# A hybrid encoder trunk on one core: unit order at the end of gate/up, a root by ScalarE, and earlier spawns

## The chip, the cores and the metric

One Trainium2 chip, one core of it. The metric is the device time of one execution in microseconds; it is taken as the median over several runs. A profile is one more execution, recorded instruction by instruction.

## The reference

One layer over 2048 tokens of width 1024, in float32. The kernel has to compute:

```python
h = rmsnorm(r, norm1_g)
proj = h @ w_in                        # q, k, v, z, beta, alpha, lx, lg
dn_out  = gated delta rule, both directions, 4 heads of 128, normed, times silu(z)
lru_out = rmsnorm(gelu(lg) * (rglru forward + rglru backward))     # 512 wide
r = r + concat([dn_out, lru_out]) @ w_out
h2 = rmsnorm(r, norm2_g)
gate = dwconv(h2 @ ffn_wg, ffn_conv_w) + ffn_conv_b                # 3 taps along the tokens, 2816 wide
r = r + (gelu(gate) * (h2 @ ffn_wu)) @ ffn_wd
pg = sigmoid(rmsnorm(r, ple_norm_g) @ ple_wg + ple_bg)
r = r + pg * (p @ ple_wp)              # p: 2048 x 256
out = rmsnorm(r, final_g)
```

## The kernel before

**A planner writes the order.** The program is a set of generators ("tasks") that a small list scheduler, `Sched`, runs while the program is built. A task yields `st(...)` with the cost that its next instruction is expected to have on an engine, `W(name)` to wait for an event that another task fires, or `M(sizes)` to wait for memory. `Sched` always takes the task whose next step could start first (plus 20 ns for each step of its priority; a lower number goes first) and issues its instructions. Each engine then executes its instructions in exactly that order. SP issues all DMAs, in order too, so a DMA that has to wait holds those issued behind it. Costs and events change only the order; on the chip, semaphores follow the data.

**Memory** is one arena of 207 KB a partition. A request is refused while there is no free block of its size, or while a task of lower priority number is waiting for memory.

**Precision.** A float32 operand is split into an f16 high and low part: ScalarE writes the high one, VectorE the low one (`split`, lines 1677 and 1679 without a scale, 1681 and 1683 with one). A product is three f16 matmuls. The large products save one in eight by a seven-product scheme: four blocks give seven operands (`operands`; three are blocks as they are, four are sums that POOL forms at line 1706), and `product` runs seven products a unit, 12 matmuls each for gate/up, 30 for down (line 1727). PSUM has banks of 128x512; each product's bank is evicted by ScalarE (line 1944) or VectorE (line 1949) for gate/up, by VectorE (line 2203) for down.

**The stages that the change touches.**

- *The output projection*, in two halves: `out_dn` over the delta rule's heads, then `out_lru` over the recurrence's 512 columns, 16 token tiles each in the order `TILES` (7, 8, 6, 9, ... 0, 15), 24 matmuls a tile (`mm`, line 456). `out_lru` has a `fetcher` that reads the rows of `catl` from DRAM with a transposing DMA (line 1622) into nine buffers. The products are added to the residual `r` by `out_add` (line 1584). The weights of each half are prepared by `out_weights` (`wprep`: loads at line 552, squares at 573 or 576, splits at 602 and 606).
- *The passage to gate/up.* `norm_pairs` takes the token tiles in eight pairs: squares by ScalarE (line 1786), the reciprocal root by `rsqrt` on VectorE alone (lines 373 to 393: an integer guess and three corrections), the scaling into `hb` (line 1794), then seven operands. Pairs 0 to 3 reach their transposed form by DMA (line 1822), pairs 4 to 7 by TensorE (`turned`, line 639) and a ScalarE copy (line 1811). `pair_weights` prepares the weights of the 22 gate/up tiles, gate (even n) and up (odd n) in turn; from n = 1 on it waits for the event `last pair`.
- *Gate/up.* `ffn` runs 44 units (n, u): weight tile pair n, half u of the tokens. `units` overlaps two units in the order 1, (3, 7 of the one before), 2, 5, (4 of the one before), 6. When both halves of gate tile pair j are there, `gate_tile` does the convolution (lines 1994, 1996, 1998) and the gelu (line 2002); `mult` multiplies by up on POOL (line 2012); `act_post` scales and splits the result and stores it to `actd` (line 2047). Three blocks of 8 KB (`blk`) hold gate and up in turn; `room` waits until the one to be written is free.
- *The seam.* At `pdone 20` (the end of unit 20, 1) four tasks start: `p_weights` prepares the 256x1024 weights of `p @ ple_wp`, and three `down_weights` tasks load `w_d` (line 2168) into one raw block of 8 KB each, take seven 2 KB pieces and split into them, one of eleven row blocks after the other. Behind gate/up `p_products` computes `p @ ple_wp` (32 groups of six matmuls; evictions at lines 2418 and 2421, stores to `ppd` at 2424), and then `down_first` runs down's first unit block by block (line 2301, 210 matmuls; `actd` loads at 2276), with 24 matmuls for the eleventh block at its end. `down_unit`'s `load` takes the 16 KB of a ring for the residual's rows when `p_products` ends.

ScalarE's functions come from tables; changing between sets shows as ACT_TABLE_LOAD rows.

Of the kernel before, what the change touches and what calls it, by code (L numbers as in the profile page):

```python
# [16 lines left out]
S = SEQ = 2048  # L17
# [284 lines left out]
def W(*name):  # L302
    return ("w", name)


def M(*sizes, high=False):
    return ("m", sizes, high)
# [48 lines left out]
class Kern:  # L356
# [11 lines left out]
    def rsqrt(self, ss, n, mul, add, outscale, y, tmp):  # L368

        nc = self.nc  # L370
        v, t = tmp[:, 0:n], tmp[:, n : 2 * n]
        yield st(dve=75 + n)
        nc.vector.tensor_scalar(v, ss, mul, add, op0=ALU.mult, op1=ALU.add)
        yield st(dve=75 + n)
        nc.vector.tensor_single_scalar(t.bitcast(I32), v.bitcast(I32), 1, op=ALU.logical_shift_right)
        yield st(dve=75 + n)
        nc.vector.tensor_scalar(y.bitcast(I32), t.bitcast(I32), -1, 0x5F3759DF, op0=ALU.mult, op1=ALU.add)

        yield st(dve=75 + n)
        nc.vector.tensor_tensor(t, y, y, op=ALU.mult)  # L380
        yield st(dve=135 + n)
        nc.vector.scalar_tensor_tensor(t, t, -0.5, v, op0=ALU.mult, op1=ALU.mult)
        yield st(dve=135 + n)
        nc.vector.scalar_tensor_tensor(y, t, 1.5, y, op0=ALU.add, op1=ALU.mult)
        yield st(dve=75 + n)
        nc.vector.tensor_tensor(t, y, y, op=ALU.mult)
        yield st(dve=75 + n)
        nc.vector.tensor_tensor(t, t, v, op=ALU.mult)
        yield st(dve=210 + 2 * n)
        nc.vector.scalar_tensor_tensor(v, t, -10.0 / 3, t, op0=ALU.add, op1=ALU.mult)  # L390
        nc.vector.tensor_scalar(y, y, 0.375 * outscale, None, op0=ALU.mult)
        yield st(dve=135 + n)
        nc.vector.scalar_tensor_tensor(y, v, 5.0, y, op0=ALU.add, op1=ALU.mult)

    def pow2_scale(self, ss, n, target, s, inv, tmp):

# [1196 lines left out]
    def out_weights(self, i):  # L1593
# [13 lines left out]
            nc.vector.tensor_scalar(w.inv, w.inv, 2.0 ** -11, None, op0=ALU.mult)  # L1607
        S.fire("wo%d" % i)

    def out_lru(self):  # L1610

        nc, S = self.nc, self.S
        n = 9
        tiles = yield M(*[2 * KB] * n)

        def fetcher():
            for j, t in enumerate(TILES):
                yield W("catl", t)
                if j >= n:
                    yield W("cat used", j - n)  # L1620
                yield ahead(1400)
                nc.sync.dma_start_transpose(tiles[j % n].f16(8, 128), self.catl[t * 128 : t * 128 + 128, :])
                S.fire("cat", j)

        S.spawn(fetcher(), PR["cat"])
        yield W("wo1")
        w = self.w["wo1"]
        for j, t in enumerate(TILES):
            yield W("cat", j)
            v = tiles[j % n].f16(8, 128)  # L1630
            yield W("r", t // 4)
            for m in range(2):
                cs = slice(m * 512, m * 512 + 512)
                pairs = [(v[:, o + k], a[:, k, cs]) for o, a in ((0, w.hi), (4, w.hi), (0, w.lo)) for k in range(4)]
                b = yield from self.mm(pairs)
                S.spawn(self.out_add(t, m, b, w.inv, "r"), 3)
            S.fire("cat used", j)
            if j + n >= 16:
                tiles[j % n].free()
        for x in self.hlo[1]:  # L1640
            x.free()
# [112 lines left out]
    def norm_pairs(self):  # L1754
# [21 lines left out]
        def begin(i):  # L1776
            ts = TILES[2 * i : 2 * i + 2]
            for t in ts:
                for m in range(2):
                    yield W("r", t, m)  # L1780
            smb = self.A.alloc(64)
            sm = smb.f32(16)
            ss, y, tmp = sm[:, 0:2], sm[:, 4:6], sm[:, 8:12]
            for k, t in enumerate(ts):
                yield st(act=c_act(D))
                nc.scalar.activation(self.junk.b16(D), self.rt(t), AF.Square, accum_out=ss[:, k : k + 1])
            yield from self.rsqrt(ss, 2, 1.0 / D, EPS, HS, y, tmp)
            (hb,) = yield M(8 * KB)
            if i == 7:
                S.fire("last pair")  # L1790
            hv = hb.f32(2, D)
            for k, t in enumerate(ts):
                yield st(dve=c_stt(D))
                nc.vector.scalar_tensor_tensor(hv[:, k], self.rt(t), y[:, k : k + 1], g, op0=ALU.mult, op1=ALU.mult)  # L1794
            smb.free()
            for t in ts:
                yield ahead(1456)
                nc.sync.dma_start(self.rd[:, t * D : t * D + D], self.rt(t))
                self.A.release(self.r[t // 4].off + t % 4 * 4 * KB, 4 * KB)
            u, o = i // 4, min(ts) % 4 * 128  # L1800
            if i % 4 == 0:
                self.hU[u] = yield M(*[8 * KB] * 7)
                S.fire("hT", u)
            yield W("hT", u)
            v = [hv[:, k, z * 512 : z * 512 + 512] for z in range(2) for k in range(2)]
            if i >= 4:
                for x in v:
                    b = yield st(pe=4 * 160, bank=1, lag=H2L)
                    P = self.turned(x, b)
                    yield st(act=c_act(512))  # L1810
                    nc.scalar.activation(x, P, AF.Copy)
                    S.release(b)

            def put(n, x):
                if i >= 4:
                    to = self.hU[u][n].f16(8, 512)[:, :, o : o + 128]
                    yield from self.split(x.rearrange("p (a n) -> p a n", n=128), to[:, 0:4], to[:, 4:8], 512)
                    return
                j, buf = yield from ring.take()
                yield from self.split(x, buf.f16(512), buf.f16(512, at=KB), 512)  # L1820
                yield st(dma=1400)
                nc.sync.dma_start_transpose(self.hU[u][n].f16(8, 512)[:, :, o : o + 128], buf.f16(1024))
                ring.done(j)

            yield from self.operands(("h2", i), RIGHT, v, 512, put)
            yield W(("h2", i), "ops")
            hb.free()
            left[0] -= 1
            if left[0] == 4:
                S.fire("h2", 0)  # L1830
            if not left[0]:
                S.fire("h2", 1)
                for x in sb + [gb]:
                    x.free()
# [66 lines left out]
    def gu_unit(self, n, u):  # L1901
# [22 lines left out]
        def room(i):  # L1924

            if x:
                k = self.rot(j)[0 if u else 2]
                if u:
                    yield W("conv", j, 0)
                else:  # L1930
                    yield W("mul", j - 1, 1) if j else W("blk")
# [131 lines left out]
    def ffn(self):  # L2063
# [15 lines left out]
        def clear():  # L2079
            for u in range(2):  # L2080
                yield W("mul", 10, u)
            for b in self.blk:
                b.free()
            yield W("act", 10)
            for b in self.ab + self.aring.bufs:
# [16 lines left out]

            return f

        todo = [(n, u) for n in range(22) for u in range(2)]
        yield from self.units([begin(n, u) for n, u in todo])
        S.fire("gu end")

# [49 lines left out]
    def down_weights(self, par):  # L2158


        nc, S = self.nc, self.S
        yield W("pdone", 20)
        (raw,) = yield M(8 * KB)
        js = RAWS[par]
        for j in js:
# [2 lines left out]
            nc.sync.dma_start(v, self.io["w_d"][256 * j : 256 * j + 256, :].rearrange("(i p) n -> p i n", p=128))  # L2168
            yield W("wd scale", 8 if j == 10 else 0)
            w = self.wd[j] = yield M(*[2 * KB] * (4 if j == 10 else 7))  # L2170
            blocks = [v[:, i, z * 512 : z * 512 + 512] for i in range(2) for z in range(2)]
            put = lambda n, x, w=w, j=j: self.split(x, w[n].f16(512), w[n].f16(512, at=KB), 512, self.asc[:, j : j + 1])
            if j == 10:
# [8 lines left out]
    def down_unit(self, i):  # L2182
# [6 lines left out]
        def load():  # L2189
            if i == 0:  # L2190
                yield W("pp end")
                self.rring = Ring(S, "r pairs", (yield M(8 * KB, 8 * KB)))
            U.n, U.r = yield from self.rring.take()
            for k, t in enumerate((i, 15 - i)):
# [192 lines left out]

    def p_weights(self):
        nc, io, S = self.nc, self.io, self.S
        yield W("pdone", 20)  # L2390
        hp = yield M(4 * KB, 4 * KB, 4 * KB, high=True)
        sg = hp.pop()
        yield from self.wprep("wp", io["ple_wp"].rearrange("(k p) n -> p k n", p=128), 2, D, None, (hp, [sg]), pieces=2)
        sg.free()
        self.wpb = hp
        yield W("phl")
        yield st(dve=80)
# [156 lines left out]
    def main(self):  # L2554
# [61 lines left out]
        S.spawn(self.p_pairs(), 9)  # L2616

        parts = (self.out_dn, self.out_lru)
        yield from parts[PARTS[0]]()

        def norms():
# [4 lines left out]
            self.mix.free()  # L2626

        S.spawn(norms(), 3)
        S.spawn(self.norm_pairs(), PR["norm"])
        S.spawn(self.pair_weights(), PR["pw"])  # L2630
        yield from parts[PARTS[1]]()
        S.spawn(self.row_squares(), 0)
        self.fsb = A.alloc(128)
# [12 lines left out]
    def go(self):  # L2646
        A, c, io = self.A, self.c, self.io
        S = self.S = Sched(A, range(2, 8))
        self.w, self.wd, self.xc, self.gl, self.zb, self.dp, self.hd, self.acc, self.act = {}, {}, {}, {}, {}, {}, {}, {}, {}
        self.rn, self.hlo, self.pw = {}, {}, {}  # L2650
        self.r, self.hU = [None] * 4, [None] * 2
        self.xT = [A.alloc(16 * KB) for _ in range(4)]
        self.junk = A.alloc(2 * KB, high=True)
# [135 lines left out]
```

## Time and profile before

| | us |
|---|---|
| median of three runs | 2758.08 (2755.16 to 2760.72) |
| the profiled execution | 2759.3 |
| its span, first to last instruction | 2757.4 |
| TensorE busy | 2561.9 (93%) |
| VectorE busy | 1867.5 (68%) |
| ScalarE busy | 1479.5 (54%) |
| GpSimd busy | 825.2 (30%) |
| granted TensorE clock, mean | 0.975 |

PE is TensorE's matmuls and PEld its weight loads, DVE is VectorE, ACT is ScalarE, POOL is GpSimd, SP is SyncE. A row of a stage gives, for each engine, busy time and the number of instructions in brackets. A row of waits gives the engine and line that waited, what released it, the sum in us, how often and the longest. A row of a group gives line, engine, operation, shapes and count, then busy time and mean ns of one, then the engine's idle time before them and what ended it. A row of the timeline gives start, duration, engine, line, and the idle time before in brackets. Busy times of small VectorE rows overlap: one is recorded until its result is written.

### The profile page before, as it was taken

Reading aid. Unit: us, or ns where it says so; the run is one execution under the profiler, and the core shown is the slowest. Engines: PE = TensorE matmul, PEld = TensorE weight load, DVE = VectorE, ACT = ScalarE, POOL = GpSimd, SP = SyncE. Lnnn points to the kernel's source line nnn. Section 1 sums busy time; section 2 is a strip of 40 time slices with the busy share of each in tenths; the row PEclk is TensorE's granted clock in tenths of the full one; section 3 lists DMA queues with packets and bytes.
Section 4 is the critical chain, followed back from the end, with each engine's and each line's share of the span. In section 5 each row is a group of like instructions: output and inputs, shape, how many; then the busy total and the mean of one; then the engine's idle time right before and its main releaser. Section 6 shows DMA issues by size and latency. Waiting matters only on the chain.

```text
span 2757.4 us, 40429 instructions
## 1 busy us (share of the span) xinstructions
PE 2561.9 (93%) x14072; PEld 1311.3 (48%) x14072; DVE 1867.5 (68%) x3902; ACT 1479.5 (54%) x3110; POOL 825.2 (30%) x618
## 2 busy tenths in 40 slices
PE   7998898898989998896999999999996799999998
PEld 4554454456656665443444444444442344444443
DVE  8668977976785667598667777778759832222458
ACT  6676677574747765245666666666646500101323
POOL 1133534736141000034345544444446400000000
PEclk9999999999999999998999999999999999999999
DMA  5332152366544468672223233333225844447973
GB/s 194 73 103 62 54 150 69 93 183 189 151 142 139 132 208 277 157 204 79 77 85 107 89 107 105 106 105 106 92 86 180 255 164 150 166 160 232 271 187 141
DMA packets 433595, 388.20 MB, mean 141 GB/s; under 512 B 158704, under 2 KB 362480, under 8 KB 433392
## 3 DMA queue, kind: packets, MB, share of 16 engines
q1 hardware_dynamic: 433392, 385.62, 46.8%
q8 instruction: 111, 1.82, 0.3%
q14 instruction: 92, 0.75, 0.1%
HBM read 230.34 MB, written 128.97 MB: 130 GB/s over the span
## 4 chain that ended last, share of the span: by engine, by line
PE 53%; DVE 6%; DMA 1%; ACT 1%; issue 1%; POOL 0%; SPq 0%; DVEq 0%; ACTq 0%
PE P L1727 40%; PE P L456 12%; DVE arena L1683 2%; DVE arena L1679 1%; PE P L2301 1%; DVE arena L1794 1%; DVE arena L1584 0%; DMA ppd<-arena 0%; DMA arena<-in_w_d_dram 0%; DMA arena<-catl 0%; DMA arena<-actd 0%; ACT arena L1681 0%; POOL arena L1706 0%; PE P L1452 0%; DVE arena L2418 0%
## 5 line engine op out<-in xcount | busy, mean ns | idle before, releaser
L1727 PE MATMUL P<-arena 128*128 128x512 f16 x5166 | 1127.2, 380 | 15.7 <-ACT arena L1944 9.8
L456 PE MATMUL P<-arena 128*128 128x512 f16 x4224 | 983.6, 384 | 32.2 <-ACT arena L2421 10.1
L1727 PEld LDWEIGHTS <-arena 128*128 128x128 f16 x5166 | 507.1, 98 | 624.1 <-issue 25.6
L456 PEld LDWEIGHTS <-arena 128*128 128x128 f16 x4224 | 413.6, 99 | 487.3 <-issue 47.0
L1683 DVE SCALAR_TENSOR_TENSOR arena<-arena 128x512 f16<-128x512 f32 (+2 forms) x408 | 449.5, 1133 | 118.6 <-ACT arena L1681 118.3
L1706 POOL TENSOR_TENSOR arena<-arena 128x512 f32<-128x512 f32 (+1 forms) x200 | 352.5, 1776 | 507.6 <-DVE arena L1683 358.4
L1681 ACT ACTIVATE arena<-arena 128x512 f16<-128x512 f32 (+2 forms) x408 | 283.0, 723 | 294.7 <-POOL arena L1706 139.8
L2203 DVE SCALAR_TENSOR_TENSOR arena<-P,arena 128x512 f32<-128x512 f32 x95 | 70.1, 750 | 225.9 <-PE P L1727 190.2
L2012 POOL TENSOR_TENSOR arena<-arena 128x512 f32<-128x512 f32 x88 | 136.3, 1569 | 241.2 <-ACT arena L2002 175.6
L2254 ACT ACTIVATE arena<-arena 128x1024 bf16<-128x1024 f32 x16 | 16.9, 1057 | 246.8 <-DVE arena L2203 237.8
L1944 ACT ACTIVATE arena<-P 128x512 f32<-128x512 f32 x176 | 102.5, 587 | 80.7 <-PE P L1727 76.1
L738 DVE SCALAR_TENSOR_TENSOR arena<-P,arena 128x511 f32<-128x511 f32 (+1 forms) x192 | 140.7, 743 | 1.9
L1261 POOL TENSOR_TENSOR arena<-arena 128x512 f32<-128x512 f32 x64 | 118.4, 1865 | 58.8 <-DVE arena L1211 46.8
L1949 DVE TENSOR_TENSOR arena<-P,arena 128x512 f32<-128x512 f32 x132 | 90.3, 684 | 36.7 <-PE P L1727 36.6
L557 POOL TENSOR_TENSOR arena<-arena 128x1024 f32<-128x1024 f32 (+1 forms) x25 | 51.7, 2072 | 198.1 <-DMA arena<-in_w_in_dram 198.1
L1459 ACT ACTIVATE arena<-P,arena 128x128 f32<-128x128 f32 x128 | 46.8, 366 | 99.4 <-PE P L1453 65.4
L1470 DVE SCALAR_TENSOR_TENSOR arena<-arena,P 128x128 f32<-128x128 f32 x128 | 43.8, 343 | 55.0 <-PE P L1465 18.5
L1464 PE MATMUL P<-arena 128*128 128x128 f32 x256 | 60.7, 320 | 17.8 <-ACT arena L1462 9.6
L1448 DVE SCALAR_TENSOR_TENSOR arena<-P,arena 128x128 f32<-128x128 f32 x128 | 44.3, 348 | 45.0 <-PE P L1446 43.6
L1164 POOL TENSOR_TENSOR arena<-arena 128x512 f32<-128x512 f32 x32 | 40.9, 1280 | 104.0 <-DVE arena L1161 96.7
L1584 DVE SCALAR_TENSOR_TENSOR arena<-P,arena 128x512 f32<-128x512 f32 x64 | 47.7, 747 | 29.8 <-PE P L456 29.6
L728 ACT ACTIVATE arena<-P,arena 128x512 f32<-128x512 f32 x64 | 44.9, 703 | 42.1 <-PE P L456 37.1
(243 smaller groups left out, 3421.3 us busy)
## 6 DMA issues: line engine op xcount, KB each, us to landing
arena<-hd SPq DMA_DIRECT2D x160, 256.0 KB, 3.2
actd<-arena SPq DMA_DIRECT2D x148, 256.0 KB, 2.5
arena<-actd SPq DMA_DIRECT2D x49, 640.0 KB, 3.9
arena<-in_w_gu_dram SPq DMA_DIRECT2D x44, 512.0 KB, 4.4
arena<-in_x_dram SPq DMA_DIRECT2D x32, 512.0 KB, 7.0
at<-arena SPq DMA_DIRECT2D x64, 256.0 KB, 2.8
arena<-at SPq DMA_DIRECT2D x128, 128.0 KB, 3.3
rd<-arena SPq DMA_DIRECT2D x32, 512.0 KB, 3.5
```

The costliest lines, as they stand in the source:

```text
L456: self.nc.tensor.matmul(out, l, r, start=(i + j == 0), stop=(i + j == m - 1))
L738: nc.vector.scalar_tensor_tensor(a[:, lo:hi], P[:, lo - sh : hi - sh], tp[:, j : j + 1], a[:, lo:hi], op0=ALU.mult, op1=ALU.add)
L1261: nc.gpsimd.tensor_tensor(pv[:, i % 2], a(slice(2 * i, 2 * i + 2)), b(slice(2 * i, 2 * i + 2)), op=ALU.mult)
L1464: nc.tensor.matmul(slot[0], k, tv[:, 2], start=True, stop=True)
L1681: nc.scalar.activation(hi, x, AF.Copy, scale=scale)
L1683: nc.vector.scalar_tensor_tensor(lo, x, scale, hi, op0=ALU.mult, op1=ALU.subtract)
L1706: nc.gpsimd.tensor_tensor(v[at], v[p], v[q], op=ALU.add if plus else ALU.subtract)
L1727: self.nc.tensor.matmul(out, l, r, start=(p in (1, 2, 5) and i + j == 0), stop=(p in (2, 3, 4) and i + j == m - 1), skip_group_check=True)
L1944: nc.scalar.activation(d, P, AF.Copy)
L1949: nc.vector.tensor_tensor(d, P, d, op=ALU.add)
L2012: nc.gpsimd.tensor_tensor(v, v, U.buf.f32(2, 2, 4, 128)[:, i, s], op=ALU.mult)
L2203: nc.vector.scalar_tensor_tensor(v, self.bank(b), self.dsm[:, at : at + 1], v, op0=ALU.mult, op1=ALU.add)
```

## The change

Three places change.

1. *The passage.* The fetcher of `out_lru` becomes a task of its own, `lru_rows`. It, `norm_pairs` and `pair_weights` are spawned before `out_dn` instead of between `out_dn` and `out_lru`.
2. *The root.* `norm_pairs` calls `rsqrt_act`: VectorE scales, ScalarE takes the square root, VectorE takes the reciprocal and does one Newton step in three instructions. Other users of `rsqrt` stay.
3. *The seam.* The last four units run in the order (20, 0), (21, 0), (20, 1), (21, 1). Unit (21, 1) gets a block of its own (`lastb`, 8 KB) and no longer waits for the convolution. `p_weights` and `down_weights` start when unit (21, 0) has issued its last product; `p_weights` has two 4 KB stages instead of one. The row ring of down waits until the blocks 8, 9 and 10 of down's weights have their memory.

```diff
+    def rsqrt_act(self, ss, n, mul, add, outscale, y, tmp):
+        nc = self.nc
+        v, t = tmp[:, 0:n], tmp[:, n : 2 * n]
+        yield st(dve=75 + n)
+        nc.vector.tensor_scalar(v, ss, mul, add, op0=ALU.mult, op1=ALU.add)
+        yield st(act=200, tab="sqrt")
+        nc.scalar.activation(t, v, AF.Sqrt)
+        yield st(dve=75 + 6 * n)
+        nc.vector.reciprocal(y, t)
+        yield st(dve=75 + n)
+        nc.vector.tensor_tensor(t, y, y, op=ALU.mult)
+        yield st(dve=135 + n)
+        nc.vector.scalar_tensor_tensor(t, t, -0.5 * outscale, v, op0=ALU.mult, op1=ALU.mult)
+        yield st(dve=135 + n)
+        nc.vector.scalar_tensor_tensor(y, t, 1.5 * outscale, y, op0=ALU.add, op1=ALU.mult)
...
+    def lru_rows(self):
+        nc, S, n = self.nc, self.S, 9
+        self.cat = tiles = yield M(*[2 * KB] * n)
+        for j, t in enumerate(TILES):
+            yield W("catl", t)
+            if j >= n:
+                yield W("cat used", j - n)
+            yield ahead(1400)
+            nc.sync.dma_start_transpose(tiles[j % n].f16(8, 128), self.catl[t * 128 : t * 128 + 128, :])
+            S.fire("cat", j)
...
-            yield from self.rsqrt(ss, 2, 1.0 / D, EPS, HS, y, tmp)
+            yield from self.rsqrt_act(ss, 2, 1.0 / D, EPS, HS, y, tmp)
...
+                if u and j == 10:
+                    if not self.lastb:
+                        self.lastb.append(None)
+                        self.lastb[:] = yield M(8 * KB)
+                        S.fire("last block")
+                    yield W("last block")
+                    U.buf = self.lastb[0]
+                    return
                 if u:
                     yield W("conv", j, 0)
...
-            for b in self.blk:
+            for b in self.blk + self.lastb:
                 b.free()
...
-        todo = [(n, u) for n in range(22) for u in range(2)]
+        todo = [(n, u) for n in range(20) for u in range(2)] + [(20, 0), (21, 0), (20, 1), (21, 1)]
...
-        yield W("pdone", 20)
+        yield W(("gu", 21, 0), "last", 4)
         (raw,) = yield M(8 * KB)
...
             w = self.wd[j] = yield M(*[2 * KB] * (4 if j == 10 else 7))
+            S.fire("wd mem", j)
...
                 yield W("pp end")
+                for j in (8, 9, 10):
+                    yield W("wd mem", j)
                 self.rring = Ring(S, "r pairs", (yield M(8 * KB, 8 * KB)))
...
-        yield W("pdone", 20)
-        hp = yield M(4 * KB, 4 * KB, 4 * KB, high=True)
-        sg = hp.pop()
-        yield from self.wprep("wp", io["ple_wp"].rearrange("(k p) n -> p k n", p=128), 2, D, None, (hp, [sg]), pieces=2)
-        sg.free()
+        yield W(("gu", 21, 0), "last", 4)
+        hp = yield M(*[4 * KB] * 4, high=True)
+        sg = [hp.pop() for _ in range(2)]
+        yield from self.wprep("wp", io["ple_wp"].rearrange("(k p) n -> p k n", p=128), 2, D, None, (hp, sg), pieces=2)
+        for b in sg:
+            b.free()
...
         parts = (self.out_dn, self.out_lru)
+        S.spawn(self.lru_rows(), PR["cat"])
+        S.spawn(self.norm_pairs(), PR["norm"])
+        S.spawn(self.pair_weights(), PR["pw"])
         yield from parts[PARTS[0]]()
...
         S.spawn(norms(), 3)
-        S.spawn(self.norm_pairs(), PR["norm"])
-        S.spawn(self.pair_weights(), PR["pw"])
         yield from parts[PARTS[1]]()
```

More of the change, by code (lines that the diff above doesn't have):

```diff
@@ L1608, in out_weights @@
         S.fire("wo%d" % i)
-    def out_lru(self):
[L1612 to L1625, printed above, removed]
+    def lru_rows(self):
[8 more added lines that the diff above has]
+            S.fire("cat", j)
+    def out_lru(self):
+        nc, S, n = self.nc, self.S, 9
         yield W("wo1")
@@ L1629, in out_lru @@
             yield W("cat", j)
+            tiles = self.cat
             v = tiles[j % n].f16(8, 128)
@@ L2649, in go @@
         self.w, self.wd, self.xc, self.gl, self.zb, self.dp, self.hd, self.acc, self.act = {}, {}, {}, {}, {}, {}, {}, {}, {}
-        self.rn, self.hlo, self.pw = {}, {}, {}
+        self.rn, self.hlo, self.pw, self.lastb = {}, {}, {}, []
         self.r, self.hU = [None] * 4, [None] * 2
```

## The prediction

> **What bounds the kernel now.** I read the busy shares first, then stages of the span, then who waited for whom in the two bad stages, then single rows there.
>
> ```profile
> span 2757.4 us, 40429 instructions
> PE 2561.9 (93%) x14072; PEld 1311.3 (48%) x14072; DVE 1867.5 (68%) x3902; ACT 1479.5 (54%) x3110; POOL 825.2 (30%) x618
> PE   7998898898989998896999999999996799999998
> ```
>
> TensorE is the bound. Only the places where its digit falls can give time, and two of them are touched: slice 19 (the passage from the output projection to gate/up) and slices 30 and 31 (the seam of gate/up and down). The stages, with busy microseconds and instruction counts:
>
> ```profile
> 1150.00:1196.00 46.00, 39.51 (x173) 17.57 (x174) 32.85 (x78) 19.06 (x35) 11.35 (x8) 0.89 0.78 173
> 1196.00:1246.00 50.00, 48.78 (x236) 23.10 (x235) 49.48 (x101) 21.78 (x40) 19.01 (x12) 1.00 0.82 212
> 1246.00:1286.00 40.00, 18.62 (x95) 11.19 (x96) 36.36 (x55) 25.62 (x50) 19.95 (x12) 0.73 0.35 110
> 2057.00:2088.00 31.00, 24.79 (x109) 10.97 (x108) 16.69 (x22) 19.65 (x25) 4.73 (x3) 0.89 0.68 217
> 2088.00:2163.00 75.00, 52.07 (x214) 21.39 (x212) 68.70 (x78) 43.62 (x67) 47.34 (x31) 0.91 0.60 189
> 2163.00:2224.00 61.00, 53.55 (x239) 23.31 (x238) 41.76 (x44) 23.91 (x36) 24.74 (x16) 0.97 0.71 226
> 2250.00:2300.00 50.00, 50.00 (x233) 22.70 (x232) 9.38 (x21) 2.30 (x4) 0.00 (x0) 1.00 0.43 139
> ```
>
> The columns are PE, PEld, DVE, ACT, POOL, granted clock, DMA share, GB/s. The last row is TensorE undisturbed: 50.00 / 233 = 0.2146 us a matmul. At that rate the three seam rows (109 + 214 + 239 = 562) need 120.6 of their 167 us, so 46.4 are lost; the three passage rows (173 + 236 + 95 = 504, some of them smaller transposes) need 108.2 of 136, so about 27.8 are lost. These are the ceilings of what the change can win. In both places VectorE is the full engine: 49.48 of 50, 68.70 of 75. The waits of TensorE in each:
>
> ```profile
> PE P L639 <- DVE arena L1794: 17.7, 3, 14.8
> PE P L456 <- DMA arena<-catl: 6.9, 1, 6.9
> PE P L456 <- ACT arena L2421: 10.1, 5, 4.5
> PE P L2301 <- DMA arena<-actd: 7.3, 3, 3.1
> PE P L1727 <- ACT arena L1944: 6.2, 1, 6.2
> PE P L1727 <- DVE arena L1949: 1.4, 1, 1.4
> ```
>
> **Part 1: the spawns of the passage.** `lru_rows` (16 transposing loads of `catl`, the same number on SP's queue as before), `norm_pairs` and `pair_weights` start before `out_dn` instead of behind it. The 6.9 us are TensorE at the start of `out_lru` with the first of these loads only just issued. Nine of sixteen now lie ahead of it: -6.9 us, bounds 0 and -6.9. On SP and DMA the same loads, the gain vector and the first weight pair move into the stretch before; they cover nothing there that TensorE waits for now, so 0. The seven splits of the first weight pair and their POOL adds also leave the passage:
>
> ```profile
> L1683 DVE SCALAR_TENSOR_TENSOR arena<-arena 128x512 f16<-128x512 f32 x7 | 6.2, 916 | 0.4 <-ACT arena L1681 0.4
> L373 DVE TENSOR_SCALAR arena<-arena 128x2 f32<-128x2 f32 x8 | 2.4, 294 | 0.9 <-ACT arena L1786 0.9
> L393 DVE SCALAR_TENSOR_TENSOR arena<-arena 128x2 f32<-128x2 f32 x8 | 1.8, 227 | 0.2
> L410 DVE RECIPROCAL arena<-arena 128x1 f32<-128x1 f32 x5 | 0.8, 163 | 0.1
> L933 ACT ACT_TABLE_LOAD  x8: 1283/1283/1283, 171.0 to 960.2; - x8
> ```
>
> **Part 2: the root.** L373 to L393 are eleven small VectorE instructions a pair, eight pairs, 25.8 us of rows in all (first and last shown). The new root has five: the first as L373 (2.4), a reciprocal (8 x 0.163 = 1.3) and three of about 2.5 each: some 11 us, so 14.5 of rows go, 11 where they don't overlap. ScalarE gets eight tiny Sqrt (no row; between 0.19, its small read rows, and 0.6, a 512-column row: I take 0.2) and two table loads of 1.283 us, one to the root's set and one back before the first gelu; it is busy 21.78 of 50, so 0, and 2.6 if that cover goes. Each pair crosses to ScalarE and back once more, behind whatever stands in its queue; I price that at 0 since the chain loses six steps, and up to 8 us if splits that wait stand ahead of it. The Trainium skill ("ScalarE: Activation LUTs", What ACT_TABLE_LOAD costs) adds a drain and gives 2.66 us a switch; two would be 5.3, still under ScalarE's idle time, and the sum would be the same.
>
> So 6.2 + 11 = 17 us of VectorE's work leaves a stretch in which it is busy 118.7 of 136. Only what lay where it was full (from 1196) reaches TensorE at once, and the last pair is held by something else:
>
> ```profile
> 1254.26 0.16 DVE L393 SCALAR_TENSOR_TENSOR arena<-arena 128x2 f32<-128x2 f32 x1
> 1273.64 2.17 DVE L1794 SCALAR_TENSOR_TENSOR arena<-arena 128x1024 f32<-128x1024 f32 x1
> ```
>
> Its root is ready at 1254.4 and its scaling comes 19 us later, behind nine splits: the pair asks for 8 KB (`hb`) when the arena has 9.1 KB in pieces of at most 4 (counted from the program's own bookkeeping). This makes the 14.8 us wait. Neither edit frees memory, so I leave that wait and take 7 of the 17: bounds 0 and -17.
>
> **Part 3: the seam.** Units now run gate 0, up 0, gate 1, up 1. What each piece does:
>
> ```profile
> 2066.40 0.74 DVE L1683 SCALAR_TENSOR_TENSOR arena<-arena 128x512 f16<-128x512 f32 x1
> 2072.50 2.35 DVE L1996 SCALAR_TENSOR_TENSOR arena<-arena 128x2047 f32<-128x2047 f32 x1 [1.59 <-ACT arena L1994]
> 2075.96 2.35 DVE L1998 SCALAR_TENSOR_TENSOR arena<-arena 128x2047 f32<-128x2047 f32 x1
> 2079.24 1.06 ACT L1944 ACTIVATE arena<-P 128x512 f32<-128x512 f32 x2
> 2079.87 9.68 PE L1727 MATMUL P<-arena 128*128 128x512 f16 x36 [6.21 <-ACT arena L1944]
> 2054.78 0.71 SPq L2168 DMA_DIRECT2D arena<-in_w_d_dram  x1
> 2067.58 1.01 SPq L2168 DMA_DIRECT2D arena<-in_w_d_dram  x2
> 2088.47 1.83 DVE L1683 SCALAR_TENSOR_TENSOR arena<-arena 128x512 f16<-128x512 f32 x1
> L1683 DVE SCALAR_TENSOR_TENSOR arena<-arena 128x512 f16<-128x512 f32 x82 | 94.4, 1199 | 10.3 <-ACT arena L1681 10.2
> ACT arena L576 <- DMA arena<-in_ple_wp_dram: 4.6, 1, 4.6
> ```
>
> The 6.2 us wait is up 1's first eviction (L1944), whose block is gate tile 0's until the convolution is through (L1998), which itself waited for the last splits of tile 9 (2066.40). `lastb` gives that unit a block of its own: the wait goes. The same convolution comes no later, since tile 9 still sets it; gate tile 1 can come up to one unit (84 x 0.2146 = 18 us) later, and only the last 24 matmuls of down's first unit need its product, so 0.
>
> By itself an earlier end of gate/up is worth little: behind it TensorE waits for VectorE (the evictions at L2421 and L2418 stand between splits). What counts is how many splits of down's weights are done before. Today the first raw block is loaded at 2054.78 and VectorE first splits it at 2088.47: the seven 2 KB pieces are refused until up 0's 56 KB come free. The new order frees them one unit earlier, at the moment that starts these tasks. 56 + 11.1 KB then hold 16 for `p_weights`, 24 raw, one set of 14 and the 8 of `lastb`; a second set must wait for 14 KB at gate 1's end. From 2057 to 2088 VectorE is idle 31 - 16.69 = 14.3 us and POOL 26. A set costs 7 x 1.199 = 8.4 us, so room is for 1.7 sets and memory for one and a half: 12 us of VectorE's work moved ahead. `p_weights` loads each piece twice today and ScalarE stands 4.6 us for the second; two stages take two loads and that wait away, inside the same 12. The row ring's 16 KB now come behind the last sets, so their two loads come later; they are needed only at the first unit's last additions, 0, or up to 7 us (the landing of such loads) if they aren't there:
>
> ```profile
> arena<-in_x_dram SPq DMA_DIRECT2D x32, 512.0 KB, 7.0
> ```
>
> I take -12 for the seam; bounds +7 and, with all waits for memory gone too, -30 of the 46.4.
>
> One rule speaks against it. First the rows: a root step of two elements takes 1.24 us while POOL adds, 0.16 elsewhere:
>
> ```profile
> 1217.68 3.94 POOL L1706 TENSOR_TENSOR arena<-arena 128x512 f32<-128x512 f32 x2 [3.75 <-DVE arena L1679]
> 1218.65 1.24 DVE L373 TENSOR_SCALAR arena<-arena 128x2 f32<-128x2 f32 x1
> ```
>
> So the sooner splits' four POOL adds a set will stretch the convolution beside them by about 1.1 us each, 4.4 a set; the convolution has no TensorE behind it any more, and the same adds no longer stretch splits later. The Trainium skill ("SBUF - State Buffer", Who interferes with whom) calls this an exclusive lock held for a whole instruction; the row agrees. By it a moved set would be worth 8.4 - 4.4 = 4 us, and the seam -6 in place of -12.
>
> **The sum.** -6.9 - 7 - 12 = -25.9 on the profiled execution's 2759.3 (span 2757.4), which is 1.2 above the median of 2758.08: 2733.4, or 2732.2 on the median. I say 2733.
>
> **The rivals.** (a) One half only: either the last pair's memory wait eats VectorE's relief and the lock halves the seam (-6.9 - 6 = -13, 2745), or the seam is paced by SP's queue, in which w_d loads that wait for a raw block stand ahead of the `actd` loads that TensorE then waits for (7.3 us). For it: the granted 4 KB pieces above. 2740 to 2750. (b) More: block places shift, the last pair gets its 8 KB at once, the 14.8 us go as well and the sets come without waits: 2733 - 15 - 8 = 2710. For it: 9.1 KB are free in sum; against it: nobody arranges that they adjoin. (c) Hidden: VectorE's order is made by a planner that reshuffles everything behind an edit; evictions fall behind the sooner splits and give it all back, 2755 to 2761. (d) Slower: the early tasks take 4 + 8 + 14 KB of the 25.1 free when the second half of w_out asks for 24. Its preparation runs
>
> ```profile
> 1034.36 0.50 SPq L552 DMA_DIRECT2D arena<-in_w_out_dram  x1
> 1096.96 1.28 DVE L606 SCALAR_TENSOR_TENSOR arena<-arena 128x1024 f16<-128x1024 f32 x1 [0.29 <-ACT arena L602]
> ```
>
> 63 us, and `out_lru` starts at 1149.6. It decides where the start slips by more than 52 us; if memory comes only when `out_dn` ends, TensorE stands the whole 63: 2733 + 63 = 2796. I count some 25 to 30 us of slip (the first pair's stage and head 3's chain free enough), so it is unlikely.
>
> **How the numbers follow.** Forecast 0.50 (own range 2722 to 2741), (a) 0.19, (b) 0.13, (c) 0.08, (d) with other losses 0.10. About 0.2%, 5.5 us, is what a measurement here can tell from no change: faster 0.82, same 0.08, slower 0.10. The range leaves out half of (b) at the low end and (d) with part of (c) at the high: 2709 to 2757.
>
> **What would show it.** No wait for `catl` at `out_lru`; five small VectorE rows a pair and one Sqrt, two table loads; no wait of L1727 for L1944 near the end of gate/up; a first split of down's weights near 2060 instead of 2088 by today's clock, and the stage from there to down's second unit 10 to 15 us shorter. It is wrong if the second w_out half is late, if the Sqrt stands behind waiting splits, or if the seam's matmuls keep today's 167 us for 562.

## The result, and the profile after

The changed kernel takes 2774.9 us (median of 6 runs, 2771.3 to 2781.8) beside 2759.4 for the kernel before: a ratio of 1.0055, interval 1.0040 to 1.0069. It is slower by 15.5 us; the forecast was 2733. Lines below 1640 have moved by 17, those behind by 17 to 29. The head of the page after, with two rows of its slices:

```profile
span 2774.3 us, 40401 instructions
PE 2566.4 (93%) x14072; PEld 1312.6 (47%) x14072; DVE 1858.6 (67%) x3854; ACT 1481.1 (53%) x3120; POOL 826.7 (30%) x618
PE   7998998998989989986999999999997899999978
PEclk9999999999999999998999999999999999999989
```

TensorE's busy time has grown by 4.5 us and the span by 16.9. The seam's digits (67 before, 78 now) have risen, the passage's 6 is still a 6, and the last digit but one has fallen from 9 to 7. That is a stage that the prediction never looked at. The waits of TensorE after, and the wait of VectorE behind the new one:

```profile
PE P L1744 <- ACT arena L1969: 27.0, 2, 22.3
PE P L473 <- DVE arena L2545: 20.7, 1, 20.7
PE P L473 <- DVE arena L2447: 8.4, 2, 5.1
PE P L2329 <- DMA arena<-actd: 6.0, 3, 3.2
PE P L656 <- DVE arena L1811: 4.8, 1, 4.8
2646.29 0.69 DVE L2551 TENSOR_TENSOR arena<-arena 128x512 f32<-128x512 f32 x1 [18.61 <-DMA arena<-ppd]
```

The forecast's part is there: the 6.9 us for `catl` and the 6.2 us for up 1's block are gone. Two waits of over 20 us are new. The first stands in the passage, in unit 0 of gate/up; the second in the last stage (`ple`, after down). To add up by place I took the start of the same TensorE instruction in each trace: from the 2534th matmul of the line L456 (L473 after) to the 1034th of gate/up for the passage, from the 3616th to the 4133rd of L1727 (L1744) for the seam, from the last of L1727 to the 3801st of L456 for the last stage. In brackets are the gaps in TensorE's rows there. Two more columns divide the passage: its length up to the 600th matmul of gate/up, and the longest wait of TensorE behind that one, which is called the second wait below:

```
                      passage        to 600th  2nd wait  seam           last stage
before                391.0 (33.2)   290.1     3.6       256.5 (36.6)    81.7  (1.6)
after                 393.1 (36.0)   291.3     4.7       246.4 (26.0)   104.9 (21.8)
e1 ppd first          391.4 (36.1)   291.1     4.5       244.6 (25.6)    81.1  (1.2)
e2 seam alone         390.6 (33.2)   289.8     3.6       246.3 (27.4)    81.1  (1.2)
e3 spawns alone       407.0 (50.1)   291.5     18.3      264.1 (42.7)    81.1  (1.2)
e4 root alone         387.2 (29.0)   285.6     4.5       259.3 (37.5)    81.1  (1.2)
e5 stage low          390.6 (34.9)   277.1     17.1      239.2 (24.1)    81.7  (1.6)
e6 blk before pair 1  384.6 (32.8)   271.3     17.7      239.2 (23.4)    81.1  (1.2)
e7 seam, ring freed   394.0 (37.9)   284.3     10.7      246.0 (27.0)    81.9  (2.0)
e8 e6, old root       395.0 (39.8)   273.9     25.4      239.3 (22.2)    81.1  (1.2)
e9 e6, conv first     386.6 (33.4)   271.3     18.3      245.8 (23.3)    81.1  (1.2)
e10 spawns and root   391.8 (36.0)   291.5     4.6       265.2 (41.6)    81.1  (1.2)
e11 e6, ring of 3     374.5 (22.7)   272.2     6.1       237.9 (20.3)    89.1  (6.3)
e12 e3, ring of 3     395.2 (39.8)   292.1     6.7       259.3 (38.2)   100.1 (17.3)
```

What lies between these stages is the same in all fourteen profiles within 0.5 us, and what follows the last within 1.7. What lies ahead of them, the first 1116 us of the kernel before, varies from 1115 to 1130 from profile to profile, with no regard to the edit (last section). Before to after: +1.2 ahead of the passage, +2.1 in it, -10.1 in the seam, +23.2 in the last stage, together +16.4 of the span's 16.9.

**Why the passage gave its gain back.** Rows of ScalarE and VectorE around unit 0 of gate/up, first before, then after:

```profile
1254.74 0.61 ACT L1944 ACTIVATE arena<-P 128x512 f32<-128x512 f32 x1
1262.92 0.58 ACT L1944 ACTIVATE arena<-P 128x512 f32<-128x512 f32 x1
1261.23 12.37 DVE L1679 TENSOR_TENSOR arena<-arena 128x512 f16<-128x512 f32 x9
```

```profile
1284.21 1.08 ACT L1969 ACTIVATE arena<-P 128x512 f32<-128x512 f32 x2 [4.98 <-DVE arena L1696]
1255.36 29.36 DVE L1696 TENSOR_TENSOR arena<-arena 128x512 f16<-128x512 f32 x22 [1.29 <-ACT arena L1694]
```

Before, unit 0's evictions stand between the splits of pairs 5 to 7. After, 22 splits run without a break and the first eviction by ScalarE stands behind them, at 1284; TensorE, which could go on from 1262.6 but needs the bank that this eviction empties, waits. The order was fixed when the program was built, by when the planner gave out memory. Counted from its bookkeeping (its own clock): in the kernel before, the 16 KB `blk` of gate/up come at 1153, ahead of the last pair's 8 KB at 1166. After, the weights' stage, `lru_rows`' buffers and the vector g, taken early, push the second half of w_out from one end of the arena into its middle, and the free space between falls into 4 KB pieces: three pairs wait for 8 KB with 17 to 29 KB free, the 56 KB of `hU[1]` come at 1152 (1148 before), and `blk`, which stands behind that request, only at 1169. The last pair gets its 8 KB at once, so its splits are all placed ahead of gate/up. And since the second pair of weights waits only for that (`last pair`), its 22 KB are granted at 1152 too, ahead of `blk`; before, they came at 1171, behind it. `blk` then gets two blocks that held pairs, so that the eviction must also wait for the splits which read them: its row has 4.98 us of idle time, ended by a split.

**What happened in the last stage.** Loads of `ppd` (the stored `p @ ple_wp`) before, after, in e1 and in e12; first and last start stand behind the durations:

```profile
L2506 SPq DMA_DIRECT2D arena<-ppd x32: 319/320/822, 2576.6 to 2727.6; - x32
```

```profile
L2535 SPq DMA_DIRECT2D arena<-ppd x32: 319/320/430, 2641.3 to 2744.2; - x32
```

```profile
L2535 SPq DMA_DIRECT2D arena<-ppd x32: 319/376/1240, 2541.2 to 2719.9; - x32
```

```profile
L2506 SPq DMA_DIRECT2D arena<-ppd x32: 319/320/431, 2651.8 to 2754.8; - x32
```

The data has lain in DRAM since the seam; only the issue is late. SP's queue is filled by two tasks of equal priority: `fetcher` (the 16 token tiles, three loads each) and `pfetcher` (`ppd`). In the kernel before `fetcher` keeps waiting for memory, and `pfetcher` gets in between. After, another distribution of free blocks delays the stage's last 4 KB row; when it comes, 60 KB are free, `fetcher` never waits, wins every tie, and puts all its 48 loads ahead of the first `ppd`, in e12 as well; before, 18 stand ahead of it, in e1 none. SP's queue after, at that place:

```profile
2636.26 3.91 SPq L2509 DMA_TRANSPOSE arena<-h3d  x2
2640.84 0.43 SPq L2511 DMA_DIRECT2D arena<-rd  x1
2641.31 1.85 SPq L2535 DMA_DIRECT2D arena<-ppd  x4
```

VectorE's L2551 then waits 18.6 us, banks stay full, TensorE stands 20.7.

### The profile page after: what moved, and what is told of

The parts are those of the page before. It is cut to its first block, busy times and chain, and to the rows that moved or that the text cites. A ratio compares the mean times of both kernels' runs of the same rounds, so it can differ in the third digit from the quotient of the medians.

```text
span 2774.3 us, 40401 instructions
## 1 busy us (share of the span) xinstructions
PE 2566.4 (93%) x14072; PEld 1312.6 (47%) x14072; DVE 1858.6 (67%) x3854; ACT 1481.1 (53%) x3120; POOL 826.7 (30%) x618
## 5 line engine op out<-in xcount | busy, mean ns | idle before, releaser
L1744 PE MATMUL P<-arena 128*128 128x512 f16 x5166 | 1124.6, 380 | 28.6 <-ACT arena L1969 27.0
L473 PE MATMUL P<-arena 128*128 128x512 f16 x4224 | 988.1, 385 | 40.1 <-DVE arena L2545 20.7
L1744 PEld LDWEIGHTS <-arena 128*128 128x128 f16 x5166 | 506.6, 98 | 636.4 <-issue 35.7
L473 PEld LDWEIGHTS <-arena 128*128 128x128 f16 x4224 | 414.6, 100 | 498.6 <-issue 67.4
L2231 DVE SCALAR_TENSOR_TENSOR arena<-P,arena 128x512 f32<-128x512 f32 x95 | 70.2, 749 | 221.6 <-PE P L1744 190.8
L2282 ACT ACTIVATE arena<-arena 128x1024 bf16<-128x1024 f32 x16 | 16.9, 1057 | 239.0 <-DVE arena L2231 230.0
L1487 DVE SCALAR_TENSOR_TENSOR arena<-arena,P 128x128 f32<-128x128 f32 x128 | 43.7, 343 | 50.1 <-PE P L1482 15.5
L2021 DVE SCALAR_TENSOR_TENSOR arena<-arena 128x2047 f32<-128x2047 f32 x22 | 51.5, 2346 | 25.2 <-ACT arena L2019 25.2
```

The source lines that it names most:

```text
L473: self.nc.tensor.matmul(out, l, r, start=(i + j == 0), stop=(i + j == m - 1))
L1744: self.nc.tensor.matmul(out, l, r, start=(p in (1, 2, 5) and i + j == 0), stop=(p in (2, 3, 4) and i + j == m - 1), skip_group_check=True)
L2231: nc.vector.scalar_tensor_tensor(v, self.bank(b), self.dsm[:, at : at + 1], v, op0=ALU.mult, op1=ALU.add)
```

## The experiments

Before's median is 2759.5 to 2761.2 in all of them; ratios are to it, with 95% intervals.

**e1.** The changed kernel, `ppd` first.

```diff
-        S.spawn(pfetcher(), 3)
+        S.spawn(pfetcher(), 2)
```

> The changed kernel with one number altered: the loader of the ple stage's `ppd` blocks runs at priority 2 instead of 3, so that it is asked before the loader of the weight tiles. Theory A (the ple stage's loss of some 23 us is an order on SP's queue: with 60 KB free the weight loader never waits for memory, and issues all its loads before the first `ppd` one): the 20.7 us wait of TensorE for VectorE's L2545 goes, and the time is 2775 - 23 = 2752. Theory B (the `ppd` loads are late for want of memory, or the late `final_g` row holds the stage): the priority changes nothing, 2775. In both the passage and the seam stay as they are in the changed kernel.

Measured 2755.1, ratio 0.9979 (0.9966 to 0.9991). The wait is gone and the last stage is back at 81.1 us. Theory A: one place in SP's queue cost 20 us of 2775, and without it the change is a gain of 0.2%.

**e2.** The kernel before with the seam's part alone (unit order, `lastb`, `p_weights` in two stages, the later row ring).

> The kernel before with the seam's part of the change alone. Theory A (the seam does what the prediction says, and the tail's loss comes from places in memory that only the whole change produces): 2759 less the 10 us that the changed kernel's seam gained, 2749; the first `ppd` load near 2570 us, as before. Theory B (the sooner splits of down's weights are what starves the ple stage): 2759 - 10 + 23 = 2772.

Measured 2749.3, 0.9959 (0.9947 to 0.9972); the seam takes 246.3 us, as in the changed kernel, and the last stage is undisturbed. Theory A.

**e3.** The kernel before with `lru_rows`, `norm_pairs` and `pair_weights` spawned early, nothing else.

> The kernel before with the three early spawns of the passage alone, the old root and the old seam. Theory A (blocks of the early tasks cut the arena into pieces, so that 8 KB blocks of three pairs and the 56 KB of the first unit come later; this eats the 9.9 us won at `catl`): 2759 - 10 + 13 = 2762, and about ten late splits of gate/up weights still between the last pair and the first eviction. Theory B (the root's trip through ScalarE's queue is what eats it): 2749.

Measured 2784.0, 1.0084 (1.0069 to 1.0099), worse than either theory. The passage loses 16 us and the old seam another 7.6. Its waits in the passage:

```profile
PE P L1727 <- ACT arena L1944: 39.0, 2, 20.7
PE P L639 <- DVE arena L1794: 11.1, 5, 5.6
```

The first of the two is unit 0's, as in the changed kernel; up to the 600th matmul this kernel is only 1.4 us behind the one before, since the wait for `catl` is gone. The second, 18.3 us at 1412, is another: a later unit's eviction waits for a convolution, and that for a block of 2 KB (e11). It makes up the other 14.6 us.

**e4.** The kernel before with `rsqrt_act` in `norm_pairs`, nothing else.

> The kernel before with the new root alone. Theory A (VectorE's small steps are not what holds the passage; the last pair's 8 KB is): 2756 to 2760, no measurable change. Theory B (the root's crossing to ScalarE costs the passage what the changed kernel lost there): about 13 us slower, 2772. The prediction's own term (VectorE's relief reaches TensorE by 7 us): 2752.

Measured 2759.9, 1.0006 (0.9994 to 1.0018): no change. Its profile has the passage 3.8 us shorter and the seam 2.8 longer.

**e10.** Both of these, the old seam.

> The kernel before with the early spawns and the new root, the old seam. Theory A (the root's shorter chain matters only beside the early spawns: up to the gate/up stage this kernel has the changed kernel's order, +3.4 us there): 2763, up to 2770 if the old seam loses what it lost in e3. Theory B (the two parts add): e3's 2784.

Measured 2770.2, 1.0039 (1.0028 to 1.0050): theory A at its upper end. Beside the early spawns the passage is 15.2 us shorter with the root (407.0 to 391.8), alone 3.8; the parts don't add. But the 15.2 don't come from VectorE's relief: up to the 600th matmul both kernels take 291.5 us, and the second wait falls from 18.3 to 4.6. By the bookkeeping the ring of 2 KB blocks that e11 is about is complete at 1274 in e3 and at 1256 here. The old seam loses 8.7 us here as in e3, which the new seam doesn't; why was not tried.

**e5.** The kernel of e1 with the stage blocks at the other end.

```diff
-                stage = yield M(4 * KB, 4 * KB, high=True)
+                stage = yield M(4 * KB, 4 * KB)
```

> The changed kernel with the `ppd` loader at priority 2, and one more word altered: the two 4 KB stage blocks of `pair_weights` are taken from the low end of the arena instead of the high end. By the program's bookkeeping the pieces then lie so that the 56 KB of `hU[1]` are granted 13 us sooner and the first units' own 16 KB (`blk`) 9 us sooner. Theory A (the passage's 22 to 23 us wait of TensorE for L1969 stands there because `blk` comes late, and the order of evictions and splits on ScalarE and VectorE is written by when it comes): the wait shrinks to about 14 and the time is 2755 - 9 = 2746. Theory B (the splits of the last three pairs are VectorE's work wherever they stand, so the place of the evictions among them is worth nothing): 2755.

Measured 2745.9, 0.9952 (0.9936 to 0.9968). The time is theory A's, but not its place: the first wait falls from 23.5 to 12.4, and a second grows from 4.5 to 17.1, so that of 14.0 us won up to the 600th matmul the passage keeps only 0.8. The rest lies mostly in the seam, 5.4 us shorter, which theory A didn't say.

**e6.** And the second weights behind `blk`:

```diff
-                yield W("last pair")
+                yield W("blk mem")
...
         self.blk = yield M(8 * KB, 8 * KB)
+        S.fire("blk mem")
```

> The kernel of the run before, and the second pair of weights asks for its 22 KB only when the first units have their 16 (`blk`). By the bookkeeping `blk` is granted 18 us sooner than in the changed kernel. Theory A (late `blk`): of the 23.5 us wait for L1969 at most 6 are left, 2755 - 17 = 2738. Theory B (VectorE's work, wherever it stands): 2755, or a little more since the second weights come later.

Measured 2738.5, 0.9926 (0.9912 to 0.9941): theory A by the total. The waits in the passage:

```profile
PE P L1744 <- ACT arena L1969: 17.7, 1, 17.7
PE P L1744 <- ACT arena L1694: 12.4, 1, 12.4
```

No eviction holds unit 0 any more, where 23.5 us stood (and 6 were foreseen). The 12.4 us stand a step later, before the first product of unit (0, 1), and are a wait for splits (L1694) of the pairs that it multiplies. Gate/up starts some 12 us sooner than in e1, the 600th matmul 19.8, and 6.8 of that last to the passage's end, because the second wait grows from 4.5 to 17.7. Only 3.3 of the 6.8 are waits in sum: TensorE's own time there (length less gaps) falls from 355.3 to 351.8. The 60 us from 1240 in e1, then in e6 (PE, PEld, DVE, ACT, POOL, then the granted clock, DMA share, GB/s):

```profile
1240.00:1300.00 60.00, 31.07 (x145) 19.04 (x146) 47.11 (x61) 33.61 (x65) 25.89 (x16) 0.72 0.39 93
```

```profile
1240.00:1300.00 60.00, 46.31 (x221) 22.25 (x220) 53.33 (x73) 38.84 (x73) 32.14 (x20) 0.89 0.24 84
```

**e7.** e2, and the pairs' ring given back early, so that the last pair has its 8 KB at once.

```diff
                 S.fire("h2", 0)
+                for x in sb:
+                    x.free()
...
-                for x in sb + [gb]:
-                    x.free()
+                gb.free()
```

> The seam's part alone, and the pairs' ring of four 2 KB blocks, which pairs 4 to 7 do not use, is freed when pair 3 is through instead of at the end. The early spawns and the new root stay out. The 8 KB adjoin, so the last pair gets its block at once. Theory A (the 14.8 us wait of the passage is want of memory, rival (b) of the prediction): the last pair's scaling comes 10 us or more sooner, the wait shrinks by 5 to 12 and the time is 2749 - 8 = 2741. Theory B (as in the changed kernel, splits that are ready sooner push the units' first evictions back and TensorE waits there instead): 2749 to 2757.

Measured 2753.9, 0.9977 (0.9964 to 0.9991), 4.6 above e2, with intervals that overlap: theory B by the time. The 14.8 us wait for the last pair is gone, and these are there:

```profile
PE P L1727 <- ACT arena L1677: 13.3, 1, 13.3
PE P L1727 <- ACT arena L1953: 10.7, 1, 10.7
```

Neither is theory B's mechanism. The 13.3 us stand before the first product of unit (0, 1), which waits for the last pairs' splits (L1677), not for an eviction; that product starts 7.7 us sooner in its stage than in e2, and the 600th matmul 5.5. The second wait, 10.7 us where e2 has 3.6, takes this back.

**e8.** e6 with the old root.

> The kernel of e6 (`ppd` loader first, stage blocks low, second weights behind `blk`) with the old root of eleven VectorE steps. By the bookkeeping `blk` comes at the same point as in e6, within 1 us. Theory A (with memory out of the way the passage is held by VectorE, and the root's some 11 us of VectorE's work reach TensorE, as the prediction's second term meant): 2738.5 + 7 to 11, about 2747. Theory B (the root is off the path, as alone in e4): 2738.5.

Measured 2748.7, 0.9957 (0.9945 to 0.9969): theory A by the total, 10.2 us more than e6, and the passage is 10.4 longer. By the place it is mostly something else: up to the 600th matmul the old root costs 2.6 us, and the second wait grows from 17.7 to 25.4. By the bookkeeping the ring is complete at 1275, in e6 at 1266. So 2.6 us is what VectorE's work is seen to cost up to there; memory was not out of the way.

**e9.** e6 with `gate_tile` at priority 1.

> The kernel of e6 with the convolution's tasks (`gate_tile`) at priority 1 instead of 2, so that they win a tie on VectorE against the splits of the next weights. In e6 TensorE waits 17.7 us at 1395 for evictions whose block is free only when a convolution is through, and the convolution's first step stands behind some twelve splits. Theory A (it is that place on VectorE): the wait falls to 4 to 8 us, as before the change, and the time to about 2728. Theory B (the tasks that are pushed back are needed as soon, and the wait appears later): 2735 to 2742.

Measured 2745.2, 0.9948 (0.9936 to 0.9959). Both theories miss: the wait stays, and the seam is 6.6 us longer. A tie on VectorE isn't what holds the convolution.

```profile
PE P L1744 <- ACT arena L1969: 18.3, 1, 18.3
```

**e11.** e6 with a ring of three:

```diff
-            self.aring = Ring(S, "act pairs", (yield M(*[2 * KB] * 4)))
+            self.aring = Ring(S, "act pairs", (yield M(*[2 * KB] * 3)))
```

> The kernel of e6 with the ring `aring` of three 2 KB blocks instead of four. In e6 the convolution of the second tile waits for the first tile's products to be written (`act`), these wait for the ring, and the ring for its fourth block, which by the bookkeeping comes only when the low task `p_pairs` has given back its 2 KB; with three blocks it is granted at once, and `act` of tile 0 comes 20 us sooner. Theory A (the 17.7 us wait at 1395 is want of 2 KB): the wait falls to 0 to 5 us, 2738.5 - 15 = 2723. Theory B (a ring of three holds the splits of the products up in all eleven tiles, or VectorE is full there): 2735 to 2745.

Measured 2737.4, 0.9915 (0.9896 to 0.9933), within the noise of e6. The wait at 1395 falls from 17.7 to 6.1, so 2 KB it was, and the passage is 10.1 us shorter. The last stage gives 8.0 back, 5.1 of them in waits of TensorE, for the splits of `ple_wg`:

```profile
PE P L473 <- ACT arena L619: 6.2, 3, 2.9
```

**e12.** e3 with a ring of three.

> The kernel of e3 (early spawns alone) with the same ring of three. In e3 the second wait of TensorE, at 1412, is 18.3 us. Theory A: that wait falls to 0 to 5, 2784 - 15 = 2769. Theory B: 2784.

Measured 2786.6, 1.0097 (1.0078 to 1.0117): theory B by the total, theory A by the place. The second wait falls from 18.3 to 6.7 and the passage by 11.8. But the last stage grows by 19.0:

```profile
PE P L456 <- DVE arena L2516: 16.1, 1, 16.1
```

This is the changed kernel's loss again, with the first `ppd` load at 2651.8, in a kernel with the old root and the old seam and no edit behind gate/up. So the loss needs neither the root nor the seam, and the early spawns alone (e3) don't bring it: it comes and goes with edits to memory in gate/up and ahead of it, some 500 us earlier and more. That it is where the blocks lie is the bookkeeping's account.

The fastest are e6 and e11, 0.7 to 0.9% under the kernel before and 1.3 to 1.4% under the change (each median against 2774.9).

## Why the prediction was wrong, step by step

Three steps failed: the 0 for what the early tasks take from others in the passage, where only queue and DMA were weighed; the 7 us of VectorE's relief by the root that were to reach TensorE; and a sum that had no term for a loss outside the two stages that the edits touch. The seam's term was right.

- **Where it looked.** "Only the places where its digit falls can give time, and two of them are touched." True for a gain. A loss can come where the digit is 9 and no edit is near: +23.2 us in `ple` against a forecast sum that has no term for it. e1 shows the cause, a place in SP's queue; e12 shows that it needs neither the root nor the seam.
- **Part 1, `catl`, -6.9.** Right: the wait is gone. The step that failed is the next: "On SP and DMA the same loads, the gain vector and the first weight pair move into the stretch before; they cover nothing there that TensorE waits for now, so 0." Queue and DMA were priced, the blocks of memory were not, though their 4 + 8 + 14 KB were counted, for rival (d) alone. In the change, blocks that come in another order put unit 0's first eviction behind 22 splits, a wait of 22.3 us; e5 and e6 change only where blocks lie and when they are asked for, and with them it shrinks to 12.4 and goes. Alone the spawns cost the passage 16.0 us (e3), 14.6 of them by the late ring.
- **Part 2, the root, -7.** Its pricing of the steps held: five steps and a Sqrt of 0.20 us, two table loads (L402, and L2027 ahead of the first gelu), and 10.4 us of VectorE's rows where 11 were said:

```profile
L400 DVE TENSOR_SCALAR arena<-arena 128x2 f32<-128x2 f32 x8 | 2.0, 246 | 0.0
L404 DVE RECIPROCAL arena<-arena 128x2 f32<-128x2 f32 x8 | 1.3, 157 | 0.3 <-ACT arena L402 0.3
L406 DVE TENSOR_TENSOR arena<-arena 128x2 f32<-128x2 f32 x8 | 3.0, 370 | 0.1
L408 DVE SCALAR_TENSOR_TENSOR arena<-arena 128x2 f32<-128x2 f32 x8 | 1.9, 231 | 0.1
L410 DVE SCALAR_TENSOR_TENSOR arena<-arena 128x2 f32<-128x2 f32 x8 | 2.2, 278 | 0.2
L402 ACT ACTIVATE arena<-arena 128x2 f32<-128x2 f32 x8 | 1.6, 203 | 11.3 <-DVE arena L400 11.2
L402 ACT ACT_TABLE_LOAD x1 | 1.3, 1283 | 0.0
```

  The switch took its 1.283 us with no idle time ahead of it (0.0 in the row), where the 2.66 us of the Trainium skill ("ScalarE: Activation LUTs", What ACT_TABLE_LOAD costs) counts a drain besides; ScalarE had room for either.

  What failed is the step from there to TensorE. Up to the 600th matmul the root is worth 4.5 us alone (e4, whose time doesn't change), nothing beside the early spawns (e10 to e3) and 2.6 with `blk` early (e8 to e6); no run shows the 7. The 15 and 10 us by which the passage differs in the last two come mostly through the ring. "So I leave that wait and take 7 of the 17" treated the last pair's wait as fixed; after, it was gone and another stood there. (Between that pair's root and its scaling lie fourteen splits, not nine.)
- **The passage in sum**: -13.9 foreseen, +2.1 measured.
- **Part 3, the seam, -12.** Right: -10.1 in the change, -10.2 alone, and 10.8 by the times of e2 (2749.3 to 2760.2). The `lastb` wait is gone. Three raw blocks are loaded from 2058.9 on, and ten splits of down's weights stand from 2067 to 2082, where before there was none until 2088; a set and a half was said. The prediction's other sum of -6, an estimate from the lock of the Trainium skill ("SBUF — State Buffer", Who interferes with whom), is further from the -10.1 that the stage shows.

```profile
2058.88 1.46 SPq L2193 DMA_DIRECT2D arena<-in_w_d_dram  x3
2076.05 2.05 DVE L1700 SCALAR_TENSOR_TENSOR arena<-arena 128x512 f16<-128x512 f32 x3
```

- **The rivals.** (c), "evictions fall behind the sooner splits and give it all back", at 0.08, is what the passage did. (b) came true in its condition and not in its result: the last pair had its 8 KB at once. In e7, where only that is added to the seam's part, 5.5 us are won up to the 600th matmul where 15 were to be won, and the second wait takes them back. (a) keeps 6.9 us of the passage, and nothing of it was kept. (d) didn't occur: w_out's second half was there and the start of `out_lru` didn't slip. None of the rivals had a loss outside passage and seam.

What stays open: why the seam is 7 to 8.5 us shorter in e5, e6, e8 and e11 than in the change (not in e9); from e1 to e5 only 1.5 of 5.4 us are gaps, the rest is TensorE's own time. The seam's four edits were not run one by one, so their shares of the 10 us are not known. What paces the splits behind the 12.4 us wait was not tried. The account of which block pushed which rests on the program's bookkeeping; that it is memory and order, e5, e6, e11 and e12 show on the chip.

## What to carry to other kernels

Where a program's own planner hands out memory and writes the order of every queue, a task that starts sooner has a price in blocks as well as in engines and queues: list who asks next for memory, in which sizes, and whether the free pieces still adjoin. Two tasks that are equal before the planner are ordered by accident; give a load that the next engine waits for its own priority, as one number did here for 20 us. And undo each part alone and in pairs before believing a part's worth, and look where the difference stands: with the same root the passage differed by 4, 10 and 15 us in three surroundings, and in the last two most of it came through a late block of 2 KB, not through the engine that the root relieved.

## What the runs showed of the hardware

The stretch ahead of the passage is the same program in e7 and in the kernel before, yet took 1130.3 and 1116.0 us in their profiles. The granted clock differs there; 200 us of it, before and in e7:

```profile
400.00:600.00 200.00, 176.62 (x1220) 96.11 (x1220) 154.75 (x315) 138.06 (x344) 101.11 (x101) 0.97 0.39 108
```

```profile
400.00:600.00 200.00, 175.60 (x1166) 95.57 (x1165) 150.48 (x303) 132.57 (x332) 95.18 (x97) 0.94 0.37 103
```

With 0.97 granted the 200 us hold 1220 matmuls, with 0.94 only 1166. Taken by the same instructions, 1219 matmuls from 400 us on last 200.1 us before and 206.6 in e7, 3.2% more, at a clock 3.3% lower (0.974 and 0.942). Over the whole stretch the gaps are nearly equal, 100.4 and 97.5 us; the difference is in the matmuls. So two single profiles can differ by 14 us with no cause in the edit; lengths of the same stage and medians are what to compare.

That a wait costs more than its length is not shown. From e1 to e6 the clock in the 60 us above rises from 0.72 to 0.89 and TensorE's own time in the passage falls by 3.5 us, but over all the runs own time doesn't follow the gaps: it is 351.8 us with e6's 32.8 us of gaps and with e11's 22.7, and 356.9 with e3's 50.1 where the kernel before has 357.8 with 33.2.
